# Expert layer of a hybrid backbone: weights in 8192-byte pieces, slot tables by scatter, down products over four banks

## The chip, the cores and the metric

The kernel runs on one core of a Trainium2 chip. The metric is the device time of one execution in microseconds. TensorE does the matrix products (PE, with its weight loads as PEld), VectorE (DVE), ScalarE (ACT) and GpSimd (POOL) the element-wise work, and SyncE (SP) issues most transfers.

## The reference, cut to what matters

One layer of a generator's backbone: 512 latent tokens of width 2048 (and 256 context tokens in the mixers) pass through three recurrent mixers and then through a mixture of experts. Only the latter is touched. Each of the 512 tokens picks one of 4 groups and in it 2 of 8 experts. An expert is a gated MLP of inner width 512.

```python
buf_tok = jnp.full((cap,), t, jnp.int32).at[dest].set(t_s)
buf_w = jnp.zeros((cap,), jnp.float32).at[dest].set(w_s)
...
xb = h_pad[idx]
return (jax.nn.silu(xb @ w_gate[e]) * (xb @ w_up[e])) @ w_down[e]
...
ys = ys.reshape(cap, d) * buf_w[:, None].astype(h.dtype)
return jax.ops.segment_sum(ys, buf_tok, num_segments=t + 1)[:t]
```

All is float32. The weights of the 32 experts are 32 x 12.58 MB = 402.65 MB, and each byte is read once.

## The kernel before

Up to about 1895 us the mixers run. Then the output projection and the routing follow (`route_setup`, `route_slots`), at 1961 us a loop over jobs for experts with more than 64 tokens (`moe_over`; its number of jobs, `njob`, is read into registers by every engine, and in these runs the loop passes with no job), and from 1964 us to the end `phase_moe`.

Every expert has 64 slots, so the experts are taken in pairs (128 slots) and gathered in fours. A "quad" below is four experts, that is two pairs.

- `load` issues the next chunk of weights from SP into one of the 10 slots of a ring, each of 8 KB per partition (1 MB). A chunk holds 256 rows of gate and of up (two transfers of 512 KB), or 256 rows of half of down (one transfer of 1 MB); a contiguous piece in memory is 4096 bytes. The order is written out in `moe_weights`; `load` is called each time that a chunk has been used.
- `gather(q)` makes the transposed tokens of four experts: the tokens, split into a high and a low part (`hh` by ACT, `hl` by DVE or POOL), times a 0/1 matrix `G`. It has eight pieces, each one PSUM bank `pc_` (four buffers).
- `slots(pr)` makes, for a pair, the 0/1 matrix `GT` from slots to tokens and the slots' weights `W`: four compares, four transposes on PE, a copy, and four small products with `rt_wm`.
- `gate_up(e)` multiplies an expert's tokens with gate and up, eight steps j; 32 products of 64 x 512 (each is two rows of the profile). Other work is put between the steps by pairs (step, call): pieces of gather, `turn` (transposes of the hidden activations), slots, `combine`.
- `down(pr, col)` multiplies the hidden activations of a pair with 512 columns of down, into one of two `py` banks; two columns after each gate_up. Then `yt`, `yeh`, `yel` scale and split the result.
- `combine()` adds one column of a pair back to the tokens: four token tiles, each two products into a `pc_` bank and one DVE add into `x1`.

PE's order is the program's order (`tc.keep_in_program_order`), so a product that waits holds back all that stands behind it:

```python
gate_up(a, *two, (1, partial(turn, a - 1)), (2, combine), (5, combine))
for col in COLS[:2]:
    down(pr - 1, col)
...
gate_up(a + 1, (0, partial(turn, a)), (1, combine), (2, partial(next, sl)), *two, (4, partial(next, sl)), (5, combine))
```

## Time and profile before

| | |
|---|---|
| three timed runs | 2987.58, 2988.66, 2991.23 us (median 2988.66) |
| the profiled execution | 2987.49 us, span 2985.7 us |
| granted clock, mean over the span | 0.963 |
| PE busy | 2722.8 us, 91% of the span |
| DVE, ACT, POOL busy | 1554.6, 842.0, 752.7 us |
| moved by DMA | 730.81 MB, mean 245 GB/s |

The page gives each engine's busy time over the whole span. Since the stages have different limits, the tables by stretch and the timeline of the expert stage are what bears on this change. A row of PE gives a run of products into one tile: its start, the time to its last product's modelled end, and their number; since products overlap, the time that a block takes is read from its start to the start of the next block.

### The profile page before, as it was taken

The numbers are of one execution on the slowest core, as the hardware profiler recorded it, in microseconds if no ns is written. First come the engines' busy times: TensorE is split into PE (matmuls) and PEld (weight loads), VectorE is DVE, ScalarE is ACT, GpSimd is POOL, SyncE is SP. The second block draws the span as 40 slices with busy tenths as digits, with TensorE's granted clock in tenths as the row PEclk, the third lists the DMA queues.
The fourth block names the chain that finished last, engine by engine and source line by source line (L and its number), as shares of the span: only waits on it lengthen the run. The fifth ranks groups of instructions, "written<-read, shape, count | busy, mean of one in ns | idle before, by whom it ended". The sixth has DMA issues, their size and how long they took to land. (4 is left out here: it accounts for less than half of the span.)

```text
span 2985.7 us, 50667 instructions
## 1 busy us (share of the span) xinstructions
PE 2722.8 (91%) x19241; PEld 1793.2 (60%) x19241; DVE 1554.6 (52%) x3183; ACT 842.0 (28%) x1638; POOL 752.7 (25%) x733
## 2 busy tenths in 40 slices
PE   5989999988899998998969888879999999999997
PEld 3468787778676776766747666744454444544533
DVE  4367566588576565565356555642343333433335
ACT  4132333346433233322222322332121221211212
POOL 2332222231344443453344343420000000000001
PEclk9999999999999999999979899989999999999999
DMA  8858787887744344443285321469999999999997
GB/s 289 304 171 244 225 254 235 241 251 234 198 105 108 94 121 101 108 127 93 74 260 163 111 91 36 132 237 409 404 408 409 407 409 408 407 410 405 409 409 290
DMA packets 527742, 730.81 MB, mean 245 GB/s; under 512 B 121137, under 2 KB 343903, under 8 KB 526339
## 3 DMA queue, kind: packets, MB, share of 16 engines
q1 hardware_dynamic: 363696, 640.77, 59.7%
q10 hardware_dynamic: 161927, 81.17, 10.7%
q0 software_dynamic: 1872, 5.57, 0.6%
q8 instruction: 155, 2.54, 0.3%
q14 instruction: 92, 0.75, 0.1%
HBM read 672.50 MB, written 54.93 MB: 244 GB/s over the span
## 5 line engine op out<-in xcount | busy, mean ns | idle before, releaser
L1691 PE MATMUL pgu<-ring,xg 128*64 128x512 f32 x2048 | 485.2, 600 | 1.9 <-DVE sil__20861 L1756 0.9
L319 POOL TENSOR_TENSOR wl<-wr,wh 128x512 fp32r<-128x512 f32 x191 | 263.1, 1378 | 701.4 <-ACT wh L318 580.9
L61 PE MATMUL pl<-hil,wh 128*128 128x512 f32 x928 | 401.4, 433 | 4.4 <-ACT hil L253 3.7
L61 PE MATMUL pl<-lol,wh 128*128 128x512 f32 x928 | 373.8, 403 | 0.2
L61 PE MATMUL pl<-hil,wl 128*128 128x512 f32 x928 | 369.8, 398 | 1.3 <-POOL wl L319 1.3
L318 ACT CAST wh<-wr 128x512 fp32r<-128x512 f32 x292 | 179.7, 619 | 583.1 <-PE pl L61 330.9
L1691 PEld LDWEIGHTS pgu<-ring,xg 128*64 128x64 f32 x2048 | 135.9, 136 | 239.0 <-issue 222.1
L1712 POOL TENSOR_TENSOR hl<-h,hh 128x512 fp32r<-128x512 f32 x32 | 41.7, 1304 | 824.8 <-ACT hh L1711 824.8
L1691 PE MATMUL py<-ring,hT 128*64 128x512 f32 x1024 | 235.9, 593 | 4.0 <-DMA ring<-in_moe_w_down_dram 4.0
L271 DVE SCALAR_TENSOR_TENSOR acc<-w,sil,acc 128x512 f32<-128x512 f32 x240 | 200.3, 866 | 56.9 <-DMA w<-in_w_ada_dram 55.8
L61 PEld LDWEIGHTS pl<-hil,wh 128*128 128x128 f32 x928 | 177.3, 191 | 58.8 <-issue 14.4
L61 PEld LDWEIGHTS pl<-hil,wl 128*128 128x128 f32 x928 | 177.4, 191 | 41.8 <-POOL wl L319 2.3
L61 PEld LDWEIGHTS pl<-lol,wh 128*128 128x128 f32 x928 | 178.2, 192 | 37.8 <-issue 6.4
L1691 PEld LDWEIGHTS py<-ring,hT 128*64 128x64 f32 x1024 | 78.7, 137 | 154.0 <-issue 135.7
L61 PE MATMUL pc<-hic,wl 128*128 128x256 f32 x496 | 145.0, 293 | 15.0 <-DVE wl L319 9.7
L61 PE MATMUL pc<-hic,wh 128*128 128x256 f32 x496 | 145.6, 295 | 4.6 <-ACT hic L253 3.2
L61 PE MATMUL pc<-loc,wh 128*128 128x256 f32 x496 | 144.5, 292 | 1.1 <-DVE loc L254 1.1
L1711 ACT CAST hh<-h 128x512 fp32r<-128x512 f32 x128 | 85.0, 665 | 165.8 <-PE pc__21215 L1691 9.0
L1712 DVE TENSOR_TENSOR hl<-h,hh 128x512 fp32r<-128x512 f32 x96 | 66.6, 694 | 119.0 <-ACT hh L1711 114.3
L1782 DVE SCALAR_TENSOR_TENSOR yt<-py,Wsl,g 128x512 f32<-128x512 f32 x64 | 48.0, 751 | 134.5 <-PE py L1691 134.5
L791 DVE TENSOR_TENSOR ptm<-Tm,Lay 64x1 f32<-64x1 f32 (+2 forms) x270 | 102.8, 381 | 27.2 <-DMA Lay<-s_ad 20.9
L1429 POOL TENSOR_TENSOR wol<-wo,woh 128x512 fp32r<-128x512 f32 x56 | 74.3, 1329 | 154.5 <-PE acc L61 94.7
(2215 smaller groups left out, 4954.7 us busy)
## 6 DMA issues: line engine op xcount, KB each, us to landing
ring<-in_moe_w_gate_dram SPq DMA_DIRECT2D x256, 512.0 KB
ring<-in_moe_w_up_dram SPq DMA_DIRECT2D x256, 512.0 KB
ring<-in_moe_w_down_dram SPq DMA_DIRECT2D x128, 1024.0 KB
wr<-in_w_in_dram ACTq DMA_DIRECT2D x288, 256.0 KB
w<-in_w_ada_dram SPq DMA_DIRECT2D x256, 256.0 KB
w<-in_w_ada_dram SPq DMA_DIRECT2D x64, 512.0 KB
wo<-in_w_out_dram SPq DMA_DIRECT2D x56, 256.0 KB
rv_xk<-d_xk SPq DMA_DIRECT2D x36, 256.0 KB
```

The costliest lines, as they stand in the source:

```text
L61: i = self.nc.tensor.matmul(*a, **k)
L271: nc.vector.scalar_tensor_tensor(acc, w, self.sil[:, k, 0:1], acc, op0=OP.mult, op1=OP.add)
L318: nc.scalar.copy(wh[:, :, :n], wr[:, :, :n])
L319: (nc.vector if q in self.wdve else nc.gpsimd).tensor_tensor(wl[:, :, :n], wr[:, :, :n], wh[:, :, :n].bitcast(F32), op=OP.subtract)
L791: nc.vector.tensor_tensor(pt_[:, :t, :t], Tm[:, :t, :t], Lay[:, :t, t].rearrange("q (o s) -> q o s", o=1).to_broadcast([64, t, t]), op=OP. ...
L1429: nc.gpsimd.tensor_tensor(wl, w, wh.bitcast(F32), op=OP.subtract)
L1691: pin(nc.tensor.matmul(*a, **k))
L1711: nc.scalar.copy(hh, h)
L1712: (nc.gpsimd if k and k0 % 4 == 0 else nc.vector).tensor_tensor(hl, h, hh.bitcast(F32), op=OP.subtract)
L1782: nc.vector.scalar_tensor_tensor(yt, py, W, self.g2[:, col[0]:sum(col)], op0=OP.mult, op1=OP.mult)
```

## The change

Gate and up come apart: a chunk is 512 rows of gate or of up, one transfer of 1 MB in pieces of 8192 bytes; gate is used at even steps j, up at odd ones, so a product has 256 columns instead of 512 and there are twice as many. The tokens' contraction rows are taken with stride 4. Down comes as 128 whole rows of 2048 columns (8192 bytes): `down(pr, (0, 1))` and `down(pr, (2, 3))` accumulate contraction tiles over four `py` banks, so all four columns of a pair end only after the second. The last pair keeps the old form (`last_down`). `pc_` gets two buffers instead of four, and a combine is issued in halves of two tiles at steps 2, 3, 4 and 5; pieces of gather are issued singly. The slots' matrices and weights come from a table `slot_tw` (token number and weight of each slot): routing computes each token's two slot addresses, eight indirect DMAs on POOL scatter (token, weight) pairs, 128 rows of 8 bytes each, into the HBM scratch `d_slot`, which SP reads back. `slots` is one compare on DVE.

```diff
+        self.d_slot = self.scratch("d_slot", [16 * P + 2 * S, 2])
+        z = op.tile([P, 16, 2], F32, name="slot0")
+        nc.gpsimd.memset(z[:, :, 0], -1.0)
+        nc.gpsimd.memset(z[:, :, 1], 0.0)
+        nc.sync.dma_start(self.d_slot[:16 * P].rearrange("(a p) c -> p a c", p=P), z)
...
+        for i, (o, ix) in enumerate(((o1, ix1), (o2, ix2))):
+            nc.vector.tensor_tensor(sp_, self.pos, o, op=OP.mult)
+            red(ad[:, :, i], sp_, OP.add)
+            nc.vector.scalar_tensor_tensor(fl[:, :, i:i + 1], ix, 64.0, ad[:, :, i:i + 1], op0=OP.mult, op1=OP.add)
+        nc.vector.tensor_scalar(in_, ad, 64.0, None, op0=OP.is_lt)
+        nc.vector.tensor_tensor(fl, fl, spare, op=OP.subtract)
+        nc.vector.tensor_tensor(fl, fl, in_, op=OP.mult)
+        nc.vector.tensor_tensor(fl, fl, spare, op=OP.add)
+        at = tp.tile([P, 8], I32, name="at")
+        nc.vector.tensor_copy(at, fl.rearrange("p t i -> p (t i)"))
+        for i in range(8):
+            nc.gpsimd.indirect_dma_start(self.d_slot[:], bass.IndirectOffsetOnAxis(ap=at[:, i:i + 1], axis=0),
+                                         tw.rearrange("p t i c -> p (t i) c")[:, i], None)
+        self.slot_tw = rp.tile([P, 16, 2], F32, name="slot_tw")
+        nc.sync.dma_start(self.slot_tw, self.d_slot[:16 * P].rearrange("(a p) c -> p a c", p=P))
...
             chunks += gu(2 * pr)
             if pr:
-                chunks += dn(pr - 1, (0,))
+                chunks += df(pr - 1, (0, 1))
             chunks += gu(2 * pr + 1)
             if pr:
-                chunks += dn(pr - 1, (1,))
+                chunks += df(pr - 1, (2, 3))
...
-            w = self.slot([P, 2, 2, 512])
-            for j, nm in enumerate(("moe_w_gate", "moe_w_up")):
-                nc.sync.dma_start(w[:, j], I[nm][0, e, 2 * c * P:(2 * c + 2) * P].rearrange("(p k) c -> p k c", k=2))
+            w = self.slot([P, 4, 512])
+            r = c // 2 * 512
+            nc.sync.dma_start(w, I[("moe_w_gate", "moe_w_up")[c % 2]][0, e, r:r + 512].rearrange("(p k) c -> p k c", k=4))
+        elif len(c) == 1:
+            w = self.slot([P, D])
+            nc.sync.dma_start(w, I["moe_w_down"][0, e, c[0] * P:(c[0] + 1) * P])
...
-                    p = ps.tile([P, 2, 256], F32, name="pc_", bufs=4)
+                    p = ps.tile([P, 2, 256], F32, name="pc_", bufs=2)
                     for k in range(2):
-                        h = self.h2[:, :, k0 * P + k:(k0 + 2) * P:2]
+                        h = self.h2[:, :, k0 // 4 * 512 + k0 % 4 + k:(k0 // 4 + 1) * 512:4]
...
             def slots(pr):
...
-                self.moe_hot(Gp, es)
-                yield
-                p = ps.tile([P, 4, P], F32, name="ts", bufs=1)
-                for t in range(4):
-                    tr(p[:, t], Gp[:, t].rearrange("p e s -> p (e s)"), self.ident)
-                nc.scalar.copy(GT, p.rearrange("p t c -> p (t c)"))
-                yield
-                pw = ps.tile([P, 2], F32, name="ts", bufs=1)
-                for t in range(4):
-                    mm(pw, Gp[:, t].rearrange("p e s -> p (e s)"), self.wm[:, t, es[0]:es[0] + 2], start=(t == 0), stop=(t == 3))
...
+                nc.vector.tensor_scalar(GT, tok, self.slot_tw[:, pr, 0:1], None, op0=OP.is_equal)
+                gts[pr] = (GT, self.slot_tw[:, pr, 1:2])
...
-                    g = wgt[e, j]
-                    for k in range(2):
+                    w = wgt[e, j]
+                    for k in range(4):
+                        kk = 4 * (j // 2) + k
                         for c in range(2):
-                            mm(p[64 * c:64 * c + 64], x[j][:, k, 64 * (e % 4):64 * (e % 4) + 64], g[:, :, k, 256 * c:256 * c + 256],
-                               start=(j == k == 0), stop=(j == 7 and k == 1), tile_position=(0, 64 * c))
+                            mm(p[64 * c:64 * c + 64, j % 2], x[kk // 2][:, kk % 2, 64 * (e % 4):64 * (e % 4) + 64], w[:, k, 256 * c:256 * c + 256],
+                               start=(j == k == 0), stop=(j == 7 and k == 3), tile_position=(0, 64 * c))
...
+            def down(pr, fs):
+
+                if fs[0] == 0:
+                    py[:] = [ps.tile([P, 512], F32, name=f"py{i}", bufs=1) for i in range(4)]
+                for f in fs:
+                    for i, col in enumerate(COLS):
+                        for c in range(2):
+                            mm(py[i][64 * c:64 * c + 64], ht[2 * pr + c][:, f % 2, 64 * (f // 2):64 * (f // 2) + 64],
+                               wgt[2 * pr + c, (f,)][:, col[0]:col[0] + 512], start=(f == 0), stop=(f == 3), tile_position=(0, 64 * c))
+                    for _ in range(2):
+                        load()
+                if fs[-1] == 3:
+                    for i in range(2):
+                        scaled(pr, i)
...
+            def combine(ts, more=True):
...
-                for t in range(4):
-                    p = ps.tile([P, col[1]], F32, name="pc_", bufs=4)
+                for t in ts:
+                    p = ps.tile([P, 512], F32, name="pc_", bufs=2)
...
+                if ts[-1] == 3:
+                    ys.pop(0)
+                    if more and i < 2:
+                        scaled(pr, i + 2)
...
+            T4 = lambda j: (j, partial(combine, (0, 1) if j % 2 == 0 else (2, 3)))
...
-                    two = () if pr % 2 else ((0, partial(next, gat)),) * 2 + ((4, partial(next, gat)),) * 2
-                    gate_up(a, *two, (1, partial(turn, a - 1)), (2, combine), (5, combine))
-                    for col in COLS[:2]:
-                        down(pr - 1, col)
+                    two = () if pr % 2 else tuple((j, partial(next, gat)) for j in (0, 1, 3, 4))
+                    gate_up(a, (0, partial(turn, a - 1)), T4(2), T4(3), T4(4), T4(5), *two)
+                    down(pr - 1, (0, 1))
+                slots(pr)
...
-                    two = ((3, partial(next, gat)),) * 2 + ((6, partial(next, gat)),) * 2
-                next(sl)
-                gate_up(a + 1, (0, partial(turn, a)), (1, combine), (2, partial(next, sl)), *two, (4, partial(next, sl)), (5, combine))
+                    two = tuple((j, partial(next, gat)) for j in (2, 3, 5, 6))
+                gate_up(a + 1, (0, partial(turn, a)), T4(2), T4(3), T4(4), T4(5), *two)
                 if pr:
-                    for col in COLS[2:]:
-                        down(pr - 1, col)
+                    down(pr - 1, (2, 3))
             turn(a + 1)
-            combine()
-            combine()
+            for j in range(4):
+                combine((0, 1) if j % 2 == 0 else (2, 3))
+            for j in range(4):
+                combine((0, 1) if j % 2 == 0 else (2, 3))

```

On POOL, at the end of the routing and the loop over jobs (`rt_wm` is the table of weights; L1604 is the load of the number of jobs into POOL's registers, L1863 the loop's branches), there stood before:

```order
L1621 TENSOR_TENSOR rt_wm<-rt_o_20102,rt_e_20172 128x128
L1622 TENSOR_TENSOR rt_me<-rt_o_20103,rt_e_20172 128x128 [waits DVE_49,Pool_49]
L1623 TENSOR_TENSOR rt_wm<-rt_wm,rt_me 128x128 [waits Pool_49]
L1604 TENSOR_LOAD njob [waits DVE_49,PE_49,Activation_49]
L1863 COMPARE_AND_BRANCH
L1863 UNCONDITIONAL_BRANCH
L1863 UNCONDITIONAL_BRANCH [waits barrier_Pool_Activation_PE_DVE_SP_gather]
```

and there stand now (`at` holds the addresses, `rt_tw` the pairs; L1610 and L1909 are the same load and branches):

```order
L1629 TENSOR_TENSOR rt_wm<-rt_wm,rt_me 128x128 [waits Pool_49]
L1648 DMA d_slot<-rt_tw,at 3072x2 [waits DVE_49]
L1648 DMA d_slot<-rt_tw,at 3072x2 [waits DMASW5_49]
L1648 DMA d_slot<-rt_tw,at 3072x2 [waits DMASW6_49]
L1648 DMA d_slot<-rt_tw,at 3072x2 [waits DMASW7_49]
L1648 DMA d_slot<-rt_tw,at 3072x2 [waits DMASW0_49]
L1648 DMA d_slot<-rt_tw,at 3072x2 [waits DMASW1_49]
L1648 DMA d_slot<-rt_tw,at 3072x2 [waits DMASW2_49]
L1648 DMA d_slot<-rt_tw,at 3072x2 [waits DMASW3_49]
L1610 TENSOR_LOAD njob [waits DVE_49,PE_49,Activation_49]
L1909 COMPARE_AND_BRANCH
```

The eight scatters stand ahead of the load of the number of jobs, and each from the second on waits for a DMA semaphore of POOL's queue.

On PE, inside the gate_up of an odd expert of a pair there stood before (`pc_` a bank of combine, `ring` a chunk, `xg` the gathered tokens, `Gp` the pair's 0/1 matrix):

```order
L1691 MATMUL pc__21586<-yeh,GT 128x512 [waits Activation_49]
L1691 MATMUL pc__21586<-yel,GT 128x512 [waits DVE_49]
L1691 MATMUL pc__21590<-yeh,GT 128x512
L1691 MATMUL pc__21590<-yel,GT 128x512
L1691 MATMUL pc__21594<-yeh,GT 128x512
L1691 MATMUL pc__21594<-yel,GT 128x512
L1691 MATMUL pc__21598<-yeh,GT 128x512
L1691 MATMUL pc__21598<-yel,GT 128x512
L1691 MATMUL pgu<-ring_21424,xg_21214 64x512 [waits DMAHW2_49,DMAHW1_49]
L1691 MATMUL pgu<-ring_21424,xg_21214 64x512 x3
L1694 MATMUL ts<-ident,Gp 128x128 [waits Activation_49]
L1694 MATMUL ts<-ident,Gp 128x128 x3
```

and now, in a gate_up with a gather, at its steps 2 and 3 (`G` marks the gather's products; each row of order is one product):

```order
L1723 MATMUL pgu<-ring_21249,xg_21288 64x256 x4
L1723 MATMUL pc__21472<-yeh,GT 128x512 [waits DVE_49]
L1723 MATMUL pc__21472<-yel,GT 128x512
L1723 MATMUL pc__21476<-yeh,GT 128x512 [waits DVE_49]
L1723 MATMUL pc__21476<-yel,GT 128x512
L1723 MATMUL pc__21487<-G,hh 128x256 [waits DVE_49]
L1723 MATMUL pc__21487<-G,hh 128x256 x3
L1723 MATMUL pc__21487<-G,hl 128x256 x4
L1723 MATMUL pc__21487<-G,hh 128x256 x4
L1723 MATMUL pc__21487<-G,hl 128x256 [waits Pool_49]
L1723 MATMUL pc__21487<-G,hl 128x256 x3
L1723 MATMUL pgu<-ring_21286,xg_21380 64x256 [waits DMAHW7_49]
```

The products with `Gp` are gone, the combine stands in halves of two tiles between steps of 8 products of 64 x 256, and a piece of gather follows a half directly and waits for DVE.

## Rows read from the trace of the kernel before

**Rows 1.** Windows: length, busy time of PE, PEld, DVE, ACT, POOL, PEclk, DMA share, GB/s.

```profile
1950.00:1967.00 17.00, 0.56 (x14) 0.45 (x14) 12.78 (x36) 4.14 (x7) 7.28 (x12) 0.50 0.38 146
...
2300.00:2400.00 100.00, 100.00 (x509) 47.71 (x509) 37.96 (x67) 20.70 (x37) 5.19 (x4) 1.00 1.02 407
```

**Rows 2.** Waits of PE and PEld, 1990 to 2986: total us, times, longest.

```profile
PE py L1691 <- DMA ring<-in_moe_w_down_dram: 4.0, 6, 1.5
...
PEld py L1691 <- DMA ring<-in_moe_w_down_dram: 13.1, 12, 2.3
```

**Rows 3.** Chain that ended last, 2260 to 2645: start, us, what.

```profile
2515.76 15.30 DMA ring<-in_moe_w_down_dram
2639.63 15.30 DMA ring<-in_moe_w_down_dram
```

**Rows 4.** DMA, 2930 to 2932 (both piece sizes) and 2938 to 2940 (4096-byte pieces).

```profile
DMA packets 160, 0.85 MB, mean 426 GB/s; under 512 B 11, under 2 KB 11, under 8 KB 101
...
DMA packets 212, 0.81 MB, mean 406 GB/s; under 512 B 14, under 2 KB 14, under 8 KB 212
```

**Rows 5.** Timeline, 1960 to 1968: start, us, engine, line, operation, out<-in, [idle <-releaser].

```profile
1960.93 0.13 DVE L1603 CAST njob<-nj 1x1 int32<-1x1 f32 x1
...
1964.05 1.43 DVE L1630 TENSOR_TENSOR G<-iota,rt_pos 128x256 fp32r<-128x256 f32 x4 [2.99 <-issue]
...
1967.73 1.20 PE L1691 MATMUL pc__20589<-G,hh 128*128 128x256 f32 x4 [7.50 <-POOL hl L1712]
```

**Rows 6.** Timeline of SP, 820 to 827: a store to HBM and the load behind it.

```profile
824.05 0.49 SPq L798 DMA_DIRECT2D s_td<-Dm  x1
...
826.23 0.86 SPq L804 DMA_DIRECT2D ed<-s_td  x2
```

**Rows 7.** DMA issues of POOL: KB each, median us from issue to landing.

```profile
gl_la<-d_la POOLq DMA_DIRECT2D x8, 384.0 KB, 3.5
...
gl_lev<-in_k_lev_dram POOLq DMA_DIRECT2D x4, 576.0 KB, 5.3
```

**Rows 8.** Timeline of PE, 2173 to 2183: the transposes and weights of a pair's slots.

```profile
2173.00 0.66 PE L1694 MATMUL ts<-ident,Gp 128*128 128x128 f32 x4
2173.58 1.94 PE L1691 MATMUL pgu<-ring,xg 128*64 128x512 f32 x8
...
2181.33 1.05 PE L1691 MATMUL ts<-rt_wm,Gp 128*128 128x2 f32 x8
```

**Rows 9.** Timeline, 2151 to 2154: one combine of four tiles, PE and DVE.

```profile
2151.89 0.50 PE L1691 MATMUL pc__21778<-yeh,GT 128*128 128x512 f32 x1
...
2152.66 0.69 DVE L1797 TENSOR_TENSOR x<-x,pc__21778 128x512 f32<-128x512 f32 x1 [4.86 <-PE pc__21778 L1691]
...
2152.92 0.39 PE L1691 MATMUL pc__21786<-yeh,GT 128*128 128x512 f32 x1
...
2153.26 0.68 DVE L1797 TENSOR_TENSOR x<-x,pc__21782 128x512 f32<-128x512 f32 x1
...
2153.93 2.37 PE L1691 MATMUL pgu<-ring,xg 128*64 128x512 f32 x10
```

**Rows 10.** Timeline of PE: a gather of two pieces, and one of one piece.

```profile
2175.45 0.73 PE L1691 MATMUL pc__21918<-G,hh 128*128 128x256 f32 x4
...
2179.46 1.94 PE L1691 MATMUL pgu<-ring,xg 128*64 128x512 f32 x8
...
1978.27 0.74 PE L1691 MATMUL pc__20678<-G,hh 128*128 128x256 f32 x4
...
1980.36 1.94 PE L1691 MATMUL pgu<-ring,xg 128*64 128x512 f32 x8
```

**Rows 11.** Matmuls with N=256, in the first stage.

```profile
61.02 1.06 PE L61 MATMUL px<-w,sil 128*32 128x256 f32 x12 [1.66 <-DMA w<-in_w_ada_dram]
```

**Rows 12.** Timeline of PE, tail: two combines.

```profile
2938.41 0.48 PE L1691 MATMUL pc__26807<-yeh,GT 128*128 128x512 f32 x1
...
2942.95 8.06 PE L1691 MATMUL py<-ring,hT 128*64 128x512 f32 x32
```

More of the change, by code (lines that the diff above doesn't have):

```diff
@@ L1639, in moe_weights @@
         dn = lambda pr, halves: [(2 * pr + i, (h, f)) for h in halves for f in range(2) for i in range(2)]
+        df = lambda pr, fs: [(2 * pr + i, (f,)) for f in fs for i in range(2)]
         for pr in range(NE // 2):
@@ L1765, in turn @@
                 del hm[e]
-            def down(pr, col):
-                W = gts[pr][1]
-                n = col[1]
-                py = ps.tile([P, n], F32, name="py", bufs=2)
+            def down(pr, fs):
[11 more added lines that the diff above has]
+                        scaled(pr, i)
@@ L1771, in down, with last_down @@
+            def last_down(pr, i):
+                col = COLS[i]
+                py[i:i + 1] = [ps.tile([P, 512], F32, name=f"py{i}", bufs=1)]
                 for f in range(4):
                     for c in range(2):
[L1773 to L1774 removed]
+                        mm(py[i][64 * c:64 * c + 64], ht[2 * pr + c][:, f % 2, 64 * (f // 2):64 * (f // 2) + 64],
+                           wgt[2 * pr + c, (col[0] // 1024, f // 2)][:, f % 2, col[0] % 1024:col[0] % 1024 + 512],
@@ L1775, in down @@
                            start=(f == 0), stop=(f == 3), tile_position=(0, 64 * c))
-                if col[0] % 1024:
+                if i % 2:
                     for _ in range(4):
                         load()
-                yt = mo.tile([P, n], F32, name="yt", bufs=1)
-                yh = mo.tile([P, n], F32R, name="yeh", bufs=2)
-                yl = mo.tile([P, n], F32R, name="yel", bufs=2)
-                nc.vector.scalar_tensor_tensor(yt, py, W, self.g2[:, col[0]:sum(col)], op0=OP.mult, op1=OP.mult)
+                scaled(pr, i)
@@ L1783, in down, with scaled @@
+            def scaled(pr, i):
+                col = COLS[i]
+                yt = mo.tile([P, 512], F32, name="yt", bufs=1)
+                yh = mo.tile([P, 512], F32R, name="yeh", bufs=2)
+                yl = mo.tile([P, 512], F32R, name="yel", bufs=2)
+                nc.vector.scalar_tensor_tensor(yt, py[i], gts[pr][1], self.g2[:, col[0]:sum(col)], op0=OP.mult, op1=OP.mult)
                 nc.scalar.copy(yh, yt)
                 nc.vector.tensor_tensor(yl, yt, yh.bitcast(F32), op=OP.subtract)
-                ys.append((pr, col, yh, yl))
@@ L1818, in phase_moe @@
                     next(gat)
-                    two = ((3, partial(next, gat)),) * 2 + ((6, partial(next, gat)),) * 2
-                next(sl)
-                gate_up(a + 1, (0, partial(turn, a)), (1, combine), (2, partial(next, sl)), *two, (4, partial(next, sl)), (5, combine))
+                    two = tuple((j, partial(next, gat)) for j in (2, 3, 5, 6))
+                gate_up(a + 1, (0, partial(turn, a)), T4(2), T4(3), T4(4), T4(5), *two)
                 if pr:
-                    for col in COLS[2:]:
-                        down(pr - 1, col)
+                    down(pr - 1, (2, 3))
             turn(a + 1)
-            combine()
-            combine()
-            for i, col in enumerate(COLS):
-                down(pr, col)
+            for j in range(4):
+                combine((0, 1) if j % 2 == 0 else (2, 3))
+            for j in range(4):
+                combine((0, 1) if j % 2 == 0 else (2, 3))
+            py[:] = [None] * 4
+            for i in range(4):
+                last_down(pr, i)
                 if i:
-                    combine()
-            combine()
+                    combine((0, 1, 2, 3), False)
+            combine((0, 1, 2, 3), False)
     def fin(self, mo, t, col):
@@ L1840, in fin @@
         sf = self.sf[:, t]
-        sq = mo.tile([P, col[1]], BF, name="sq3", tag="Gp", bufs=1)
+        sq = mo.tile([P, col[1]], BF, name="sq3", tag="hl", bufs=2)
         nc.scalar.activation(sq, x[:, cs], AF.Square, accum_out=sf[:, b:b + 1])
@@ L2050, in tail @@
             fin()
+            next(r)
             next(r, None)
```

36 lines of the change are left out of this document (18 added, 18 removed).

## The prediction

> **What bounds the kernel now.** I read the busy time by stretch first. In the expert stage PE is busy through the whole of a window and the DMA share is 1.02 at 407 GB/s [rows 1]; the windows from 2000 to 2900 all read like this one. Two resources are full at once, so the waits must say which gives way. They are small: all PE idleness put to the loads of down is 4.0 us, and that of its weight loads 13.1 us in 12 waits [rows 2]. The chain of waits passes through one DMA of down per quad, 123.87 us apart [rows 3]. A quad's weights are 4 x 12.58 = 50.3 MB, which 407 GB/s moves in 123.6 us. So transfers and PE are in balance to about 1%: a faster transfer alone gains the PE's waits, no more, and PE work that is removed alone gains little either. Only both together would shorten a quad.
>
> **Pieces of 8192 bytes.** In two windows of the tail, the one in which a load of 8192-byte pieces is under way with the 4096-byte ones moved 426 GB/s, the one with 4096-byte pieces alone 406 [rows 4]. So 4 to 5% of transfer time, some 119 us a quad instead of 123.6. That is now below PE's time, and the load waits go: between 4.0 and 17.1 us of [rows 2]; I take -14, since a chain that goes through a load in every quad points to the upper end.
>
> **The scatter before the loop.** The rows of order in the section on the change show POOL's eight scatters in a chain, each waiting for the semaphore of the one before, ahead of POOL's load of the number of jobs; the loop's branches wait for all engines. So PE, DVE, ACT and SP stand until the last has landed. Before, the number of jobs was ready at 1960.93, DVE made `G` at 1964.05 and PE began the gather at 1967.73 [rows 5]; PE had next to nothing to do from 1950 on [rows 1], so a delay here hides behind nothing, and the ring is full at PE's start in either version. First come some 11 short DVE operations, between 0.13 (the cast) and 0.36 us (a quarter of the 1.43) [rows 5]; at 0.23 the addresses are ready at about 1963.4. No scatter stands in this trace. From below: SP's store to HBM was issued at 824.05 and the load that reads it went at 826.23 [rows 6], so at most 2.2 us for a store by the hardware queue. From above: POOL's own loads took 3.5 and 5.3 us to landing, at 384 and 576 KB each [rows 7]. A scatter moves 1 KB but needs POOL to make its descriptors; it is nearer to the store, and I take 2.7 us. 8 x 2.7 = 21.6, so the chain ends at 1985.0; with the same 3.1 us to `G` this is 1988.1, **+24 us**. The ends are 8 x 2.2 = 17.6 (+20) and 8 x 5.3 = 42.4 (+45).
>
> The Trainium skill ("DMA: Bandwidth & Descriptors", section on the anatomy of one DMA on the SWDGE path) gives a fixed cost of about 2.0 us for each such DMA, most of it the receipt from the memory written to, HBM being the heaviest. By it the chain is an estimated 16 us and the sum would be 5.6 us lower; the store of [rows 6] allows that figure, POOL's loads of [rows 7] lie above it.
>
> The zeroing of `d_slot` (one small transfer, some 60 us earlier) and the read-back, which is SP's first transfer after the loop, are hidden: the first use of the table comes a whole gate_up later.
>
> **Slots.** Four transposes with `Gp` took 0.58 us of PE's time to the next product, the weights' products 1.05 less the same 0.08 of overlap, 0.97 [rows 8]. 16 pairs: 16 x 1.55 = **-24.8 us**. DVE has a compare of 128 x 512 in place of four small ones; it is idle most of the time [rows 1].
>
> **Combine in halves.** Four tiles took 2153.93 - 2151.89 = 2.04 us; the third tile's products began 1.03 us after the first's, and the change to the next product adds about 0.1 [rows 9], so a half takes 1.13 and two halves 2.26. 56 of the 64 columns stand between steps: 56 x 0.22 = **+12.3**.
>
> **Single pieces of gather.** Two pieces together took 4.01 us, one alone 2.09 [rows 10]: +0.17 a pair of pieces, 28 such pairs after the first quad, **+4.8**.
>
> **256 columns instead of 512.** A step of 8 rows takes 1.87 us now (2173.58 to 2175.45 [rows 8, 10]), 0.43 for two concurrent rows plus one break of 0.15. The only f32 products of 256 columns in column groups span 1.06 - 0.38 = 0.68 us from first to last start for three intervals [rows 11], 0.227 at most against 0.215 for half of 0.43; the span includes the stagger of the last group. So 0 to 5%; I take 1% of 256 steps x 1.87 = 479 us, **+4.8**, ends 0 and +24.
>
> **Two banks instead of four.** After the change a gather piece can follow a half combine at once. DVE's add of the half's first tile starts 0.77 us after the tile and lasts 0.69 [rows 9]; the bank is free at 1.46, PE is through with the half at 1.13 and waits 0.33, with the semaphore 0.4. Gather stands at steps 0, 1, 3, 4 of the even gate_up and 2, 3, 5, 6 of the odd one, halves at 2 to 5 in both, so this happens to five of eight pieces a quad, 35 times: **+14**. From below it is nothing, if DVE is earlier; from above 1.0 us each, if DVE is one more operation of 0.69 behind: +35.
>
> **Tail.** A pair's four columns now end together, so gate_up(3) has no combine (-2 x 2.04 = -4.1) and four stand behind the last gate_up instead of two, in two banks, at DVE's pace of 0.60 a tile [rows 9]: 16 x 0.60 + 0.77, and two columns' scaling between, two operations of about 0.69 each, 2.8: 13.2 us where two combines took 4.54 [rows 12], +8.7. The last three combines of four tiles wait about 0.5 each for banks, +1.5. Together **+6.1**.
>
> **Sum.** -14 + 24 - 24.8 + 12.3 + 4.8 + 4.8 + 14 + 6.1 = +27.2. On the profiled execution's own 2987.5 this is 3014.7; the median of the runs lies 1.2 higher, so I predict **3015 us**, +0.9%. A change of 0.2%, 6 us, is about what a measurement of this kernel tells from none.
>
> **Rivals.**
> *Transfers set the pace after all* (faster). If PE's full windows are in truth a PE that follows the loads, the stage falls with the bytes: 402.65 MB at 407 are 989 us, at 426 945, -44; the scatter's +24 stays, so 2968. For it speaks the DMA share above 1 and the load in the chain of every quad [rows 1, 3]. Against it, 2.0 to 2.1 us for a piece of gather and 0.215 us a row are the same wherever I look, and waits are named for 17 us at most [rows 2]. It decides if PE's own blocks come out shorter. In this direction points the Trainium skill's "DMA: Bandwidth & Descriptors", section Measured, whose largest transfer reaches 425 GB/s where this stage has 407; the page does not say what a full PE does with it. Chance 0.12.
> *Low ends together* (faster, or none): the scatter at 2.2 (-4), no bank waits (-14), no loss to 256 columns (-4.8) leave +4.4, about 2993; with a half combine that costs no more than half of a whole (-12.3) it is 2981. Chance 0.16, half of it within 0.2%.
> *Slow landing* (much slower): each scatter 5.3 us; +45 for +24 gives 3036, with the bank waits at 1.0 us 3057. POOL's loads speak for it, the 1 KB against. Chance 0.17.
> *The forecast*, slower by the chain with PE's savings spent on halves and banks, 2995 to 3045: 0.55.
>
> **The numbers.** Faster 0.12 + 0.08 = 0.20, within 0.2% 0.08, slower 0.72. The range cuts a tenth at each end: from between the first rival and the low ends, 2972, to between the forecast's end and slow landing with bank waits, 3048.
>
> **What the profile would show.** Scatter: PE's first gather at about 1992 instead of 1967.73, all engines idle before it, POOL's scatters 2.7 us apart. Transfers: about 425 GB/s while they run, a share below 1 in the windows from 2100 on, and no load in the chain. Banks: waits of `pc_<-G,hh` for the DVE add, 0.4 us each. Columns: 8 rows of 64 x 256 in half the time of 8 rows of 64 x 512. Quads within 1 us of the 123.87 of before, but without the wait for a load. The prediction is wrong if the scatters land in less than 1 us each, or if a quad takes under 121 us.

## The result, and the profile after

The changed kernel takes 3020.8 us (median of four runs, 3013.56 to 3030.71) against 2989.94 for the kernel before beside it: a ratio of 1.0096, 95% interval 1.0075 to 1.0117. Run once more unaltered it is 3022.46 against 2992.95, 1.0109 (1.0075 to 1.0143). The forecast was 3015 us and slower.

The profiled execution took 3013.56 us, span 3011.8. It is read in three stretches, each beside the same one of before.

**Ahead of the experts.** The timeline of all engines (start, length, engine, line, operation):

```profile
1959.96 0.13 DVE L1609 CAST njob<-nj 1x1 int32<-1x1 f32 x1
...
1962.72 1.15 POOL L1648 DMA_INDIRECT d_slot<-rt_tw,at  x1 [3.63 <-DVE at L1646]
1969.27 0.97 POOL L1648 DMA_INDIRECT d_slot<-rt_tw,at  x1 [5.40 <-DMA d_slot<-rt_tw,at]
1971.76 0.96 POOL L1648 DMA_INDIRECT d_slot<-rt_tw,at  x1 [1.52 <-DMA d_slot<-rt_tw,at]
...
1984.13 0.96 POOL L1648 DMA_INDIRECT d_slot<-rt_tw,at  x1 [1.40 <-DMA d_slot<-rt_tw,at]
...
1987.59 1.43 DVE L1658 TENSOR_TENSOR G<-iota,rt_pos 128x256 fp32r<-128x256 f32 x4 [25.17 <-issue]
...
1989.74 1.22 PE L1723 MATMUL pc__20617<-G,hh 128*128 128x256 f32 x4 [30.48 <-DMA slot_tw<-d_slot]
```

The number of jobs is ready at 1959.96, a microsecond earlier than in [rows 5]; the addresses take DVE to 1962.4. Then POOL issues a scatter, waits for its landing, issues the next. The second stands 6.55 us behind the first, the others 2.4 to 2.9 us apart. SP had issued its last two loads of 1 MB at 1961, and from 1963 to 1967 the transfers ran at 406 to 414 GB/s; in a version below in which no load is under way, the first scatter lands in 3.1 us. DVE's `G` and PE's first gather come 23.5 and 22.0 us later than in [rows 5]; from the number of jobs to the gather it is 29.8 us instead of 6.8, **+23.0**. The groups of PE's waits say the same in one row; the semaphore that came last there is that of the read-back, but the chain had held everything until then:

```profile
PE pc__20617 L1723 <- DMA slot_tw<-d_slot: 30.5, 1, 30.5
...
PE py L1723 <- DMA ring<-in_moe_w_down_dram: 0.8, 1, 0.8
```

A smaller cost lies further ahead, in the output projection: there PE waits for DVE, and DVE for weights of the projection (DVE's wait is 5.9 us where it was 4.1), while SP's zeroing of `d_slot`, issued at 1876, is under way. A mark ahead of that wait is PE's last product into `acc`. Its row of the timeline, and the row of PE's waits from 1870 to 2000 (total, times, longest), first before the change, then after it:

```profile
1889.40 0.39 PE L61 MATMUL acc<-wol,yh 128*128 128x512 f32 x1
PE g L61 <- DVE x L1435: 3.1, 2, 2.6
```

```profile
1885.14 0.39 PE L61 MATMUL acc<-wol,yh 128*128 128x512 f32 x1
PE g L61 <- DVE x L1435: 5.3, 3, 4.5
```

From the mark to the number of jobs it is 71.5 us before and 74.8 now, **+3.3**: PE's longest wait is 1.9 us longer, and from 1890 to 1898, behind it, the granted clock is 0.65, where it was 1.00.

**The quads.** The loads now wait for PE, which the row on down above shows from PE's side: 0.8 us of waiting for down where [rows 2] had 4.0. The windows have a DMA share near 1 still, and move between 398 and 420 GB/s, where [rows 1] had 407 at 1.02 (columns as there):

```profile
2100.00:2200.00 100.00, 98.58 (x666) 56.81 (x667) 37.87 (x55) 18.75 (x27) 4.82 (x3) 1.00 1.01 420
2300.00:2400.00 100.00, 98.45 (x674) 58.09 (x672) 39.03 (x54) 26.24 (x34) 6.36 (x4) 1.00 0.98 401
```

The chain of waits holds no load in this stretch; its longest pieces are PE's own products of down, one of which comes back after 124.26 us, a quad:

```profile
2211.27 6.87 PE py L1723 x32
...
2335.53 6.87 PE py L1723 x32
...
2459.80 6.87 PE py L1723 x32
```

In PE's timeline a piece of gather directly behind a half combine waits for DVE's add, and one behind a step of gate/up does not:

```profile
2348.20 0.74 PE L1723 MATMUL pc__23140<-G,hh 128*128 128x256 f32 x4
...
2355.21 0.50 PE L1723 MATMUL pc__23194<-yeh,GT 128*128 128x512 f32 x1
...
2356.03 0.40 PE L1723 MATMUL pc__23198<-yel,GT 128*128 128x512 f32 x1
2356.73 0.75 PE L1723 MATMUL pc__23209<-G,hh 128*128 128x256 f32 x4 [0.31 <-DVE x L1838]
```

Summed over four quads from PE's rows, each block from its start to the start of the next (so that a wait counts to the block ahead of it), the two kernels spend:

```
us in four quads        before (2269.82 to 2764.95)  changed (2335.36 to 2832.47)
gate/up                 235.0                        234.3
down                    111.9                        109.9
combine                  65.4 (whole, 2.04 each)      80.5 (halves, 1.26 each)
gather                   64.4 (pairs, 4.02 each)      67.3 (single, 2.10 each)
slots                    12.6                          0
hidden turned             5.9                          5.2
```

What the slots gave (12.6) and the loads gave (2.1) went into the halves of combine with the waits behind them (15.1) and the gather (2.9); in all the four quads are 2.0 us longer.

**The tail.** Four combines in two banks stand behind the last gate/up. PE's timeline:

```profile
2956.06 0.48 PE L1723 MATMUL pc__27281<-yeh,GT 128*128 128x512 f32 x1
...
2958.75 0.50 PE L1723 MATMUL pc__27293<-yeh,GT 128*128 128x512 f32 x1 [0.47 <-DVE x L1838]
...
2969.81 7.09 PE L1723 MATMUL py<-ring,hT 128*64 128x512 f32 x32
```

They take 2969.81 - 2956.06 = 13.75 us where two took 4.54 [rows 12], with PE waiting for DVE's adds. From down's first product behind the last gate/up to the end it is 64.8 us (2947.02 to 3011.8) instead of 57.7.

So the 26.1 us between the two spans are: the mark in the output projection 4.3 earlier, from it to the number of jobs +3.3, the scatter +23.0, the first gather +0.9, from the first gate/up product to the first down behind the last gate/up -3.9 (951.6 to 947.7), the tail +7.1. From the mark on it is +30.4, close to the 30.9 between the medians.

A caution for all that follows. The stages ahead end at different times in different executions: the mark above stands between 1883 and 1903 us in the fourteen profiles. The runs of one kernel spread over some 20 us, those of before too (2976.2 to 3003.3 in all), which fits. For what a part does I therefore give, beside the ratio, the time from the number of jobs to the end of the profiled execution ("job to end"): 1024.8 us before, 1051.8 and 1049.2 changed (the second from the run that follows). It leaves out what the zeroing costs ahead of it.

### The profile page after: what moved, and what is told of

It reads as the page before. It is cut to its first block, busy times and chain, and to the rows that moved or that the text cites. A ratio compares the mean times of both kernels' runs of the same rounds, so it can differ in the third digit from the quotient of the medians.

```text
span 3011.8 us, 53816 instructions
## 1 busy us (share of the span) xinstructions
PE 2717.9 (90%) x21097; PEld 1909.5 (63%) x21097; DVE 1588.1 (53%) x3114; ACT 891.8 (30%) x1622; POOL 777.0 (26%) x747
## 5 line engine op out<-in xcount | busy, mean ns | idle before, releaser
L1723 PE MATMUL pgu<-ring,xg 128*64 128x256 f32 x4096 | 484.8, 383 | 2.1 <-DVE sil__21004 L1777 0.9
L1723 PEld LDWEIGHTS pgu<-ring,xg 128*64 128x64 f32 x4096 | 279.7, 137 | 180.4 <-issue 48.1
L1744 POOL TENSOR_TENSOR hl<-h,hh 128x512 fp32r<-128x512 f32 x32 | 51.0, 1593 | 810.9 <-ACT hh L1743 810.9
L1723 PE MATMUL py<-ring,hT 128*64 128x512 f32 x1024 | 227.3, 592 | 0.8 <-DMA ring<-in_moe_w_down_dram 0.8
L1743 ACT CAST hh<-h 128x512 fp32r<-128x512 f32 x128 | 141.0, 1148 | 141.8 <-PE pc__24696 L1723 5.8
L1744 DVE TENSOR_TENSOR hl<-h,hh 128x512 fp32r<-128x512 f32 x96 | 105.5, 1114 | 105.0 <-ACT hh L1743 105.0
L319 DVE TENSOR_TENSOR wl<-wr,wh 128x512 fp32r<-128x512 f32 x101 | 75.6, 750 | 75.4 <-ACT wh L318 74.8
L1823 ACT CAST yeh<-yt 128x512 fp32r<-128x512 f32 x64 | 39.7, 620 | 248.8 <-DVE yt L1822 117.4
```

The source lines that it names most:

```text
L319: (nc.vector if q in self.wdve else nc.gpsimd).tensor_tensor(wl[:, :, :n], wr[:, :, :n], wh[:, :, :n].bitcast(F32), op=OP.subtract)
L1723: pin(nc.tensor.matmul(*a, **k))
L1743: nc.scalar.copy(hh, h)
L1744: (nc.gpsimd if k and k0 % 4 == 0 else nc.vector).tensor_tensor(hl, h, hh.bitcast(F32), op=OP.subtract)
L1823: nc.scalar.copy(yh, yt)
```

## The experiments

**The changed kernel again.** No edit.

> The changed kernel once more, unaltered, as the reference for the three runs beside it and for the spread of its times (3013.6 to 3030.7 us in four runs, against 2987.6 to 2992.4 for the kernel before). Theory: median 3014 to 3025, ratio 1.009, the first gather on PE at about 1990 us, eight scatters 2.4 us apart but the first 6.5. Rival for the spread: it belongs to the chip and not to the kernel; then the kernel before spreads as wide here.

Measured: 1.0109 (1.0075 to 1.0143), the gather at 1990.16, the scatters as before (6.35 us, then 2.4). The kernel before spread from 2979.83 to 3000.57 in the same session, so the rival for the spread holds.

**Eight tables, no chain.**

```diff
+        self.d_slot = [self.scratch(f"d_slot{i}", [16 * P + 2 * S, 2]) for i in range(8)]
...
-            nc.gpsimd.indirect_dma_start(self.d_slot[:], bass.IndirectOffsetOnAxis(ap=at[:, i:i + 1], axis=0),
+            nc.gpsimd.indirect_dma_start(self.d_slot[i][:], bass.IndirectOffsetOnAxis(ap=at[:, i:i + 1], axis=0),
...
+                    nc.vector.tensor_reduce(self.slot_tw[:, :, 0], s8[:, :, 0], axis=mybir.AxisListType.X, op=OP.max)
+                    nc.vector.tensor_reduce(self.slot_tw[:, :, 1], s8[:, :, 1], axis=mybir.AxisListType.X, op=OP.add)
```

> Each of the eight scatters writes a table of its own in HBM, so none waits for the landing of another; eight tables are read back and merged by two reductions on DVE. Theory (the chain of landings costs 23 us): POOL issues all eight in 8 x 1.1 = 9 us from 1962.7, the last lands 2.4 to 6.5 us later, the gather starts at about 1978 to 1981 instead of 1990: 9 to 12 us faster than the changed kernel. Rival (the delay is absorbed, as the transfers set the pace afterwards): the gather starts as early, but the end moves by less than 3 us.

Measured: 1.0167 (1.0121 to 1.0213), slower than the changed kernel by some 24 us, against both expectations. The profile parts it. Job to end is 1038.3 us, 11 to 13.5 less than the changed kernel; from the number of jobs to the gather 18.0 instead of 29.8 and 29.0. POOL's timeline shows scatters 1.3 us apart, none waiting for the one before:

```profile
2011.64 1.15 POOL L1649 DMA_INDIRECT d_slot<-rt_tw,at  x1 [3.63 <-DVE at L1647]
2013.09 0.97 POOL L1649 DMA_INDIRECT d_slot<-rt_tw,at  x1 [0.30 <-issue]
...
2020.67 0.96 POOL L1649 DMA_INDIRECT d_slot<-rt_tw,at  x1 [0.30 <-issue]
```

But the number of jobs was ready only at 2008.87, 115.7 us behind the mark instead of 74.8. The groups of PE's waits, 1870 to 2000, and the timelines of DVE and SP name the place: in the output projection PE waited 31 us for DVE, and DVE 32 us for weights to arrive, while SP was busy for 31.5 us with eight transfers that zero the tables, 2048 pieces of 8 bytes each. In the two stretches of 20 us behind the wait the granted clock was 0.71 and 0.55, where the changed kernel had 0.86 and 1.00, which lengthens the routing further:

```profile
PE g L61 <- DVE x L1435: 31.5, 3, 30.8
```

```profile
1921.68 1.29 DVE L1465 TENSOR_TENSOR w<-w,gt 128x512 f32<-128x512 f32 x2 [32.21 <-DMA w<-in_w_out_dram]
```

```profile
1884.18 31.50 SPq L1514 DMA_DIRECT2D d_slot<-slot  x8
```

**Eight tables, zeroed in 128-byte pieces.** Since every row of a table starts equal, the zeroing may go by any layout.

```diff
-                nc.sync.dma_start(d[:16 * P].rearrange("(a p) c -> p a c", p=P), z)
+                nc.sync.dma_start(d[:16 * P].rearrange("(p a) c -> p a c", p=P), z)
```

> The eight tables without a chain again, with the zeroing in 128 pieces of 128 bytes a table instead of 2048 of 8; with those, the first form's eight zeroing transfers held the output projection up by some 30 us. Theory (from the number of jobs to the end the chain's absence gave 12 us, the zeroing took them away ahead of it): 10 to 14 us below the changed kernel, that is 14 to 20 us above the kernel before. Rival (the later start came from something else): the output projection is as late as in the first form.

Measured: 1.0052 (1.0033 to 1.0071), 17 us above the kernel before beside it. As the theory had it, and against the rival. SP's eight zeroing transfers take 5.44 us instead of 31.50, PE's longest wait in the projection is 2.8 us, near the 2.6 of the kernel before, and job to end is 1038.2, as in the first form:

```profile
1883.87 5.44 SPq L1514 DMA_DIRECT2D d_slot<-slot  x8
```

The chain is worth 11 to 13.5 us of the 23; what is left there is the addresses, eight issues of 1.26 us and the last landing, still ahead of the loop.

With this the cost of one zeroing can be read too. From the mark to the number of jobs it is 70.8 to 71.5 us in the three profiles of kernels that zero nothing, 70.6 to 73.0 in the five with one table zeroed in 128-byte pieces, and 74.5 to 74.9 in the four with one table in 8-byte pieces: some 3 us.

**The chain behind the loop.** The eight scatters stay chained, but are written behind the loop of jobs, in `phase_moe`, and POOL reads the table back on its own queue.

```diff
+            self.scatter()
...
-                        (nc.gpsimd if k and k0 % 4 == 0 else nc.vector).tensor_tensor(hl, h, hh.bitcast(F32), op=OP.subtract)
+                        (nc.gpsimd if q and k and k0 % 4 == 0 else nc.vector).tensor_tensor(hl, h, hh.bitcast(F32), op=OP.subtract)
...
-                slots(pr)
+                if pr == 1:
+                    slots(0)
+                if pr:
+                    slots(pr)
```

> The same chain of eight scatters, issued by POOL behind the loop of overflow jobs instead of ahead of it, with the read-back on POOL's own queue; the first quad's low parts are made by DVE alone, since POOL is taken. Theory: nothing waits for the chain until the first scaling of down near 2080 us, the gather starts at about 1968 again, and the time is 20 to 23 us below the changed kernel, within 5 us of the kernel before. If the scatters' landing makes the spread, it shrinks to that of the kernel before. Rival (absorbed): less than 8 us below the changed kernel.

Measured: 1.0068 (1.0044 to 1.0092), only 5.6 us less than the changed kernel beside it by medians; job to end 1037.8, 12.7 less. The gather starts 9.4 us after the number of jobs instead of 29.8 and 29.0, and then some 7 us are lost again. The 9.4 are not quite the 6.8 of before: in the trace POOL issues the first scatter still ahead of the loop, at 1979.62, and its landing, 3.1 us later, is on the chain of waits there; the other seven come behind. The timelines of DVE and of PE show most of the 7 us: two compares of `slots` stand early in DVE's order and wait for the read-back, and the last piece of the first gather waits behind them.

```profile
2017.04 0.88 DVE L1762 TENSOR_SCALAR GT<-tok,slot_tw 128x512 fp32r<-128x512 f32 x2 [7.31 <-DMA slot_tw<-d_slot]
```

```profile
2018.95 1.22 PE L1727 MATMUL pc__20857<-G,hl 128*128 128x256 f32 x4 [4.62 <-DVE hl L1748]
```

**The same, without the side costs.** The compares are pinned to their place behind the third gate/up, and the zeroing goes in 128-byte pieces.

```diff
-                nc.vector.tensor_scalar(GT, tok, self.slot_tw[:, pr, 0:1], None, op0=OP.is_equal)
+                pin(nc.vector.tensor_scalar(GT, tok, self.slot_tw[:, pr, 0:1], None, op0=OP.is_equal))
```

> The late scatter again, with two of its side costs taken away: DVE's compares of the first pairs stay behind the third gate_up (in the first form they had been moved ahead on DVE, waited 7.3 us there for the read-back, and PE waited 4.6 us behind them), and the zeroing writes 128 pieces of 128 bytes instead of 2048 of 8. Theory: from the number of jobs to the end 1051 - 20 - 2 = about 1029 us, with the first form's 4.6 us gone; in all 22 to 27 us below the changed kernel, level with the kernel before. Rival (what is left of the slowdown is more than the front): still 10 us or more above the kernel before.

Measured: 1.0016 (0.9997 to 1.0034), job to end 1029.3. As the theory had it. The front was nearly all of the slowdown: with it hidden, the change as a whole costs nothing that this comparison can tell, though job to end is still 4.5 us above the kernel before. Quads are 124.27 us as before the edit.

**Gather away from the halves, two pieces in a row.**

```diff
-                    two = () if pr % 2 else tuple((j, partial(next, gat)) for j in (0, 1, 3, 4))
+                    two = () if pr % 2 else tuple((j, partial(next, gat)) for j in (0, 0, 1, 1))
...
-                    two = tuple((j, partial(next, gat)) for j in (2, 3, 5, 6))
+                    two = tuple((j, partial(next, gat)) for j in (0, 1, 6, 7))
```

> The changed kernel with no gather piece directly behind a half combine: two pieces at each of steps 0 and 1 of the even gate_up, and one each at 0, 1, 6 and 7 of the odd one; two banks as before. Theory (a piece waits 0.37 us for the DVE add that frees its bank, 35 times): those waits go, a quad shortens from 124.27 by 1.8 us, 11 to 13 us in all. Rival (the bank is only the first of several waits; with stride 4 ACT's cast of the high part takes 1.15 us instead of 0.67, and closely spaced pieces wait for it): less than 4 us.

Measured: 1.0077 (1.005 to 1.0105), 3 us less than the changed kernel by medians; job to end 1046.4, 3 to 5 less; quads 123.5 to 123.9, 0.5 less on the mean. The theory's waits are gone, and the rival's have come: in PE's timeline the second of two pieces in a row waits for its low part.

```profile
2361.88 0.64 PE L1723 MATMUL pc__23103<-G,hl 128*128 128x256 f32 x4
2362.36 0.75 PE L1723 MATMUL pc__23130<-G,hh 128*128 128x256 f32 x4
2363.47 0.74 PE L1723 MATMUL pc__23130<-G,hl 128*128 128x256 f32 x4 [0.36 <-DVE hl L1744]
```

**The loads alone, on the kernel before.** Gate and up in 8192-byte pieces, so 256 columns and stride 4 in the gather; everything else as before.

```diff
-            w = self.slot([P, 2, 2, 512])
...
+            w = self.slot([P, 4, 512])
...
-                        h = self.h2[:, :, k0 * P + k:(k0 + 2) * P:2]
+                        h = self.h2[:, :, k0 // 4 * 512 + k0 % 4 + k:(k0 // 4 + 1) * 512:4]
```

> The kernel before with one part alone: gate and up apart in 8192-byte pieces, so 256 columns a product and stride 4 in the gather; slots, four banks, down and combine as before. Theory (transfers and PE in balance; faster transfers give only the waits for loads, 10 to 14 us, and 256 columns take some back): 4 to 12 us below the kernel before, quads near 123 us, the load share below 1. Rival (transfers set the pace): two thirds of the bytes 4% faster, quads of 120 us, 25 to 29 us below.

Measured: 1.0096 (1.0069 to 1.0124), 28 us slower than the kernel before, against both. Job to end 1051.4, quads of 126.8 to 127.7. The gate/up blocks are as long as before to 1% (236.4 us in four quads), but a double piece of gather takes 4.80 us instead of 4.02. ACT's groups, 2100 to 2900, first of this kernel, then of the kernel before, give the reason:

```profile
L1711 ACT CAST hh<-h 128x512 fp32r<-128x512 f32 x94 | 101.6, 1130 | 114.4 <-PE pc__23993 L1691 8.3 <-PE pc__25787 L1691 8.3 <-PE pc__22199 L1691 8.3
```

```profile
L1711 ACT CAST hh<-h 128x512 fp32r<-128x512 f32 x94 | 62.5, 665 | 127.9 <-PE pc__22016 L1691 9.0 <-PE pc__25220 L1691 9.0 <-PE pc__26021 L1691 9.0
```

A cast that reads every fourth float takes 1130 ns, one that reads every second 665. I had priced the stride at nothing. The loads gained nothing meanwhile: they ran at 397 GB/s over a quad, and SP's longest waits, in total, were for slots of the ring that PE had not yet freed.

**The loads alone, gather in single pieces.**

```diff
-                    two = () if pr % 2 else ((0, partial(next, gat)),) * 2 + ((4, partial(next, gat)),) * 2
+                    two = () if pr % 2 else tuple((j, partial(next, gat)) for j in (0, 1, 3, 4))
...
-                    two = ((3, partial(next, gat)),) * 2 + ((6, partial(next, gat)),) * 2
+                    two = tuple((j, partial(next, gat)) for j in (2, 3, 5, 6))
```

> The loads alone on the kernel before (gate and up in 8192-byte pieces), now with the gather's pieces issued singly, as the changed kernel does. Alone with double pieces this part cost 28 us: a double piece took 4.80 us instead of 4.02, since with stride 4 ACT's cast takes 1.15 us instead of 0.67 and two pieces in a row wait for it, and the ring starved meanwhile. Theory (the casts are the cause): a single piece takes 2.1 us, quads fall from 127 to about 124, and the time is within 6 us of the kernel before. Rival (the loads themselves, larger and in bursts with down's, are the cause): quads stay at 126 or more, 15 us or more above the kernel before.

Measured: 1.0022 (1.0004 to 1.004), 2996.24 against 2987.53. A single piece takes 2.08 us, quads are 124.5 to 125.7. The casts were the cause of most of the 28 us; the time, 8.7 us above the kernel before, is 3 us outside what the theory gave, and quads are no shorter than before: larger pieces alone give nothing here.

**The slots alone, on the kernel before.** The table scattered behind the loop; no transposes and products with `Gp`.

```diff
-                    tr(p[:, t], Gp[:, t].rearrange("p e s -> p (e s)"), self.ident)
...
+                pin(nc.vector.tensor_scalar(GT, tok, self.slot_tw[:, pr, 0:1], None, op0=OP.is_equal))
```

> The kernel before with the slots' table alone: scattered behind the loop of jobs, read back on POOL's queue, no transposes and no weights' products on PE; loads of 4096-byte pieces, four banks, down and combine as before. Theory (balance): PE loses 3.1 us of work in a quad, the loads then set the pace at 123 us and PE waits for them; within 6 us of the kernel before. Rival (PE alone sets the pace): quads of 120.5 us, 20 us below.

Measured: 1.0003 (0.9987 to 1.002), job to end 1026.0, as the theory had it. PE does 12.6 us less in four quads and waits as much more for down: the blocks of down take 125.7 us there instead of 111.9. PE's waits from 1990 to the end, where [rows 2] had 4.0:

```profile
PE py L1723 <- DMA ring<-in_moe_w_down_dram: 21.1, 22, 1.6
```

**Both, on the kernel before.** The loads (with double pieces of gather) and the slots together.

```diff
+            w = self.slot([P, 4, 512])
...
+                        h = self.h2[:, :, k0 // 4 * 512 + k0 % 4 + k:(k0 // 4 + 1) * 512:4]
...
+            self.scatter()
...
+                pin(nc.vector.tensor_scalar(GT, tok, self.slot_tw[:, pr, 0:1], None, op0=OP.is_equal))
```

> Both parts together on the kernel before: gate and up in 8192-byte pieces and the slots' table scattered late; four banks, down and combine as before. Theory (only both together shorten a quad): PE 122.8 - 3.1 + 0.4 = about 120 us a quad, loads about 120: 15 to 25 us below the kernel before, more than the two parts apart give together. Rival (one of the two was the bound alone): no better than the better of the two parts.

Measured: 1.004 (1.0015 to 1.0065), 12 us above the kernel before where the theory had 15 to 25 below; job to end 1044.6: better than the loads alone, worse than the slots alone, as the rival had it. Quads are 123.6 to 128.7 us. Double pieces again take 4.80 us, and PE waits 16.2 us for down.

**Both, gather in single pieces.** As in the loads alone:

```diff
...
-                    two = ((3, partial(next, gat)),) * 2 + ((6, partial(next, gat)),) * 2
+                    two = tuple((j, partial(next, gat)) for j in (2, 3, 5, 6))
```

> Loads in 8192-byte pieces, single gather pieces and the slots' table scattered late, on the kernel before with its four banks, whole combines and old down. Theory: PE 122.8 - 3.1 + 0.5 + 0.7 = 121 us a quad, loads 120 to 121, so quads of 121 to 122 and 10 to 18 us below the kernel before. Rival (bursts of four down loads of 4096-byte pieces hold the loads up): quads of 124 or more, no better than the kernel before.

Measured: 1.0009 (0.9989 to 1.0028), against the theory. Quads are 122.8 to 125.5, PE waiting for the loads of down, which still come in 4096-byte pieces and four at a time, as the rival had it (PE's waits, 1990 to 2930):

```profile
PE py L1723 <- DMA ring<-in_moe_w_down_dram: 13.8, 14, 1.5
```

**Late scatter, and the gather spread out.** The late scatter without side costs; gather and halves never share a step, and no two pieces follow each other.

```diff
-                    two = () if pr % 2 else tuple((j, partial(next, gat)) for j in (0, 1, 3, 4))
-                    gate_up(a, (0, partial(turn, a - 1)), T4(2), T4(3), T4(4), T4(5), *two)
+                    two = () if pr % 2 else tuple((j, partial(next, gat)) for j in (0, 1, 2, 3))
+                    gate_up(a, (0, partial(turn, a - 1)), T4(4), T4(5), T4(6), T4(7), *two)
...
-                    two = tuple((j, partial(next, gat)) for j in (2, 3, 5, 6))
+                    two = tuple((j, partial(next, gat)) for j in (0, 1, 6, 7))
```

> The late scatter (with late compares and zeroing in 128-byte pieces) and, beside it, no gather piece behind a half combine and no two pieces in a row: gather at steps 0 to 3 and halves at 4 to 7 of the even gate_up, gather at 0, 1, 6 and 7 and halves at 2 to 5 of the odd one. Theory (a bank wait of 0.41 us five times a quad): quads fall from 124.27 to 122.2 to 122.6, 12 to 16 us less than the late scatter alone, which puts it 6 to 12 us below the kernel before; the first place where loads and PE both end sooner. Rival (another wait takes its place: casts at stride 4, the fourth bank of down behind halves at step 7, or loads): quads of 123.6 or more, within 6 us of the kernel before.

Measured: 0.9983 (0.997 to 0.9997), 2982.8 us against 2984.64: the one version below both kernels, by 1.8 us where 6 to 12 were expected, at the edge of what can be told. Quads are 122.8 us, a half combine takes 1.14 us instead of 1.26, and the chain of waits repeats through PE's own gate/up blocks:

```profile
2383.67 7.06 PE pgu L1727 x64
2506.50 7.06 PE pgu L1727 x64
2629.31 7.06 PE pgu L1727 x64
```

Job to end is 1021.2, 8 below the late scatter alone where 12 to 16 were expected. The halves' blocks give back 1.9 us a quad, as the theory had it, of which the other blocks take 0.4: quads are 1.46 shorter.

## Why the prediction was right

- **The scatter before the loop**: +24 forecast, +23.0 measured. The step held as it was written, a chain of landings with every engine behind it. The sizes inside differ: mostly 2.4 us a scatter where I took 2.7, but the first took 6.55, behind two loads of 1 MB. Eight tables without a chain, and the chain behind the loop, took 11 to 12 and 20 us off between the number of jobs and the gather. Under the cover of the experts' work the seven scatters behind the loop cost nothing that the comparison can tell. The Trainium skill ("DMA: Bandwidth & Descriptors", anatomy of one DMA on the SWDGE path) puts a fixed 2.0 us on each; this case's trace shows 2.4 to 2.9 us from issue to issue in six of seven, so the page is near, and the chain is what makes it a cost.
- **Transfers and PE in balance**: right. Slots alone moved 12.6 us of PE's work into waits for loads; loads alone, the gather's price apart, gave nothing; the rival in which transfers set the pace (2968 us) is out. The sign of a DMA share below 1 came only in part: it is 0.98 to 1.01, at 398 to 420 GB/s instead of 425.
- **Slots** -24.8: 12.6 us in four quads, 25 in all. **Combine in halves** +12.3: 1.14 us a half where nothing waits, against 1.13. **Single pieces** +4.8: 2.9 us in four quads, 5 in all.
- **Two banks instead of four** +14: five of sixteen halves in a quad are 0.38 us longer, by PE's wait of 0.31 us and the start behind it; that is 7.5 us in four quads, 13 in all. Moving the gather away gave back 1.46 us a quad of that, or 0.5 where the pieces then stood in a row.
- **256 columns** +4.8: mis-sized, it is nothing (234.3 us in four quads against 235.0). Of the 0 to 5% that [rows 11] left open, with the stagger of the last group in it, the low end held.
- **Load waits** -14: mis-sized, about half. Down's blocks shrink by 2.1 us in four quads, 3.2 in all up to the last gate/up, and in the tail by 3.5 (8.85, 7.01 and 3.58 us instead of 10.23, 7.99 and 4.69), 6.7 together. That is nearer to the 4.0 us that PE itself waited than to the 17.1 with the waits of its weight loads added, which the forecast leaned towards. The second quad still takes 125.4 us.
- **Tail** +6.1: four combines 13.75 us (forecast 13.2), each of the last three in two banks 0.75 longer (0.5); with gate_up(3) without its combines about +7.4.
- **The stride of the gather** had no term. In the changed kernel it is hidden by single pieces; ahead of the first gate/up, where pieces follow each other and PE waits for low parts, the gather is 0.9 us longer. Without single pieces it is 0.78 us for each pair of pieces.
- **The zeroing** I called hidden, and gave it no term. It was not: one table costs 3.3 us in the output projection, eight cost a wait of 31. Here the forecast was wrong in kind: a small transfer was taken to cost nothing because its result is needed late, and it held up another transfer that DVE and PE stood behind.

That the sum came so near is in part luck: 256 columns (5.4 us less than forecast) set off most of the load waits (7.3 more). The median lies 6 us above the forecast, of which 3.3 are the zeroing. The profiled execution (3013.56) lies 1 us below it only because its mark stood 4.3 us earlier than in the profile of before; ahead of the mark executions differ by more than that.

What stays open: why loads in 8192-byte pieces with the old down still hold PE up at 122.8 to 125.5 us a quad. In the chain of waits there (2200 to 2700) a load of down takes 19.5 to 20.1 us, and 18.2 to 19.0 with the loads alone and single pieces, where the kernel before and the slots alone have 15.3. That the bursts of four down loads do it is argued from the late version with down by contraction tiles, which waits for no load between 2100 and the tail; down alone was not tried. So it is not shown which part of the new loads lets the last version's quads end sooner.

## What to carry to other kernels

A scratch table in HBM that is written in pieces costs a landing for each piece if the writes follow each other; the place of the chain decides whether it costs anything, so it belongs behind work that doesn't need it, with nothing early in another engine's order that waits for it. A table that is zeroed in very small pieces can hold up other transfers far from where it is used. Where transfers and an engine are both full, relieving one moves its time into waits for the other, so a change must relieve both and must not spend what it saves on PE in change-overs and banks; the one version here that came out below the kernel before gained 1.8 us. When a load's layout changes, price the element-wise work that reads with the new stride, not only the transfer.

## What the runs showed of the hardware that was not expected

- A cast of 128 x 512 floats on ACT took 665 ns reading every second float and 1130 to 1149 ns reading every fourth; DVE's subtraction 692 and 1114 ns (680 for rows without a stride, in the output projection). The Trainium skill ("SBUF — State Buffer", section on the DMA port swizzle) says that accesses which share a 16-byte line run at full rate and each new line pays; these rows agree with that: two reads a line at stride 2, one at stride 4.
- A transfer of 16 KB in 2048 pieces of 8 bytes: eight of them kept SP's queue busy for 31.5 us, in 128-byte pieces 5.44, and DVE waited 32.2 us for a weight load of ACT's queue beside them, 4.1 us in the kernel before; one of them cost the kernel some 3 us.
- A scatter of 128 rows of 8 bytes took 2.4 to 2.9 us from issue to the next issue with nothing else under way, and 6.4 to 6.6 behind two loads of 1 MB.
- At a DMA share of 1.01 the loads ran at 412 to 420 GB/s in 8192-byte pieces, and in 4096-byte pieces at 407 at 1.02 [rows 1].
